# A decoder layer on one core: the embedding's projection moved from behind the output projection to the start and kept in DRAM, and the MLP's first two tiles cut by tokens around LN1's last transposes

## The chip, the cores and the metric

One core of a Trainium2 chip runs the kernel. The metric is the time of one execution on the device, in microseconds (us). TensorE (PE) multiplies, VectorE (DVE) and ScalarE (ACT) work element by element, GpSimd (POOL) does the small odd things and starts the accumulating transfers, and SyncE (SP) starts most other transfers between DRAM and the on-chip memory (SBUF). PE's results land in PSUM banks, from which DVE and ACT read them.

## The reference, cut to what matters

One layer on 512 tokens of width 1024, all in float32:

```python
h = layer_norm(x, ln_in_g, ln_in_b)
pool_in, qkv, z, beta, a, gate_a, gate_b = split(h @ w_in)
y_a = multiscale_pool(pool_in) ; y_b = gated_deltanet(qkv, z, beta, a)
mixed = sigmoid(gate_a) * y_a + sigmoid(gate_b) * y_b
h = layer_norm(alpha * h + mixed @ w_out, ln1_g, ln1_b)
r = alpha * h + square(relu(h @ w_up)) @ w_down
ple = sigmoid(r @ ple_gate_w) * (p @ ple_proj_w)
out = layer_norm(r + ple, ln2_g, ln2_b)
```

The change concerns `p @ ple_proj_w`: `p` is the token embedding (512 x 256), `ple_proj_w` is 256 x 1024. This product needs nothing but inputs and is first used in the last step but one.

## The kernel before

Float32 values are split into a high part that PE multiplies fast and a low part, and each product is three matmuls: high by high, high by low, low by high. A weight slab of 512 KB is loaded by SP into a `raw` buffer (three of them), ACT casts it to `hi`, DVE subtracts to get `lo` (`load`, lines 48 to 59; four buffers of each). `load` runs these two ahead of their turn, by `high_priority`. Activations live feature by feature in `act`, 8 blocks of 128 features by 512 tokens, high and low.

Until the MLP a scheduler orders each engine's instructions by the program's order and the priorities given; `issue_after` forces an order between two of them. From the MLP on, everything goes through the wrappers `oT`, `oV`, `oA`, `oS`, `oG`, which keep the order of the code on each engine.

**The start (lines 137 to 254).** PE runs 14 warm-up matmuls on the identity. SP loads `x` as eight halves of 256 KB (four tiles of 128 tokens), then the first weights. For each tile DVE takes the statistics (`stats`, lines 98 to 103), POOL works out the scale, and ACT normalises in place (line 213). PE transposes feature block by feature block (`ps_in`, line 228); behind two of these in block 3 stand four more warm-up matmuls. ACT applies gain and offset (`hf_in`, line 233), and ACT or DVE writes the high part, DVE the low part (lines 234, 235). PE then multiplies these features by the small beta/decay weights (`ps_ba`, lines 247 and 248) and the first k weights (`ps_k`, lines 66 to 68). `ps_bat` (line 254) follows the last of `ps_ba`.

**The middle.** Projections, DeltaNet by pairs of heads, pool mixer and gates follow. At lines 735 to 743 the token embedding is loaded (`ptok`), transposed by PE and split into `pT`. `tok_gemm` (from line 749) multiplies the mixed result by `w_out`; its callback `out_done` (from line 796) adds the residual, takes LN1's statistics, applies the norm into `res[t]`, and calls `to_features` (lines 109 to 119), which transposes `res[t]` into `act` through PSUM tiles `ps_l`. Behind `tok_gemm` stands the embedding's projection (lines 814 to 826): two weight halves, eight PSUM tiles `ps_pp`, 48 matmuls, and eight ACT copies into SBUF tiles `pproj`, where they stay until the end.

**The MLP (from line 831).** Eight chunks `c` of 512 hidden features. A chunk has four tiles of the up projection (`up_tile`), each 24 matmuls over all 512 tokens. Only the first two tiles of chunk 0 are cut into token halves, `HALVES`, 48 matmuls of 256 columns each. `even_block` and `odd_block` apply the squared ReLU on ACT and split it into `hid_a`, `hid_b` and `hid_s` on ACT and DVE. The down projection is a Strassen-like scheme with seven products of 2 x 2 blocks. Its right-hand sides are sums of quarters of `w_down`, built in place: `fetch` loads a quarter (`x`, `y`, `z`, `w`), and `onto` adds the next quarter onto it by an accumulating transfer that POOL issues, after ACT and DVE have split the former content (`split_dn`: `hi_dn` on ACT, `lo_dn` on DVE). In chunk 0 ACT also scales the four residual tiles (`alpha_h`). All lines that go through the wrappers carry the number 844 in the profile.

**The end.** After chunk 7 the last products are gathered into `res`, `features` transposes `res` into `act` (`ps_rt`), `gate_tile` multiplies by `ple_gate_w` (`ps_pg`), `embed` multiplies the sigmoid by `pproj`, and `finish` does LN2 and the output.

Of the kernel before, what the change touches and what calls it, by code (L numbers as in the profile page):

```python
# [33 lines left out]
def layer(tc, x, p, ln_in_g, ln_in_b, w_in, pool_w, pool_scale, conv_w, a_log, dt_bias, o_norm_w,  # L34
# [163 lines left out]


# [25 lines left out]
    for kb in range(KB):  # L225
        ps = pp1.tile([P, SEQ], F32, tag=("tp", "sc")[kb % 2], bufs=2, name=f"ps_in_{kb}")
        for t in range(NT):
            pe_last = T.transpose(ps[:, t * P:(t + 1) * P], xts[t][:, kb * P:(kb + 1) * P], ident)
# [505 lines left out]

    ptok = tp2.tile([P, NT, 256], F32, tag="ptok", bufs=1, name="ptok")
    dma(out=ptok, in_=p[0, 0].rearrange("(t p) c -> p t c", p=P))
    pT = tp2.tile([P, 2, 2, SEQ], F32R, tag="pT", bufs=1, name="pT")
    for kb in range(2):
        ps = pp2.tile([P, SEQ], F32, tag="tp", bufs=2, name=f"ps_pT{kb}")
        for t in range(NT):  # L740
            T.transpose(ps[:, t * P:(t + 1) * P], ptok[:, t, kb * P:(kb + 1) * P], ident)
        A.copy(pT[:, kb, 0, :], ps)
        V.tensor_tensor(out=pT[:, kb, 1, :], in0=ps, in1=pT[:, kb, 0, :].bitcast(F32), op=SUB)

# [68 lines left out]

    pproj = {}
    for half in range(2):
        hi, lo = load(ple_proj_w[0, :, 512 * half:512 * half + 512].rearrange("(a p) c -> p a c", p=P), 512,
                      f"pp{half}")
        for t in range(NT):
            ps = pp2.tile([P, 512], F32, tag="g", bufs=pp2g, name=f"ps_pp{half}{t}")
            for kb in range(2):  # L820
                ah, al = pT[:, kb, 0, t * P:(t + 1) * P], pT[:, kb, 1, t * P:(t + 1) * P]
                T.matmul(ps, ah, hi[:, kb, :], start=kb == 0, stop=False)
                T.matmul(ps, ah, lo[:, kb, :], start=False, stop=False)
                T.matmul(ps, al, hi[:, kb, :], start=False, stop=kb == 1)
            pproj[t, half] = ep.tile([P, 512], F32, tag="E", bufs=8, name=f"pproj{half}{t}")
            A.copy(pproj[t, half], ps)
# [345 lines left out]
```

## Time and profile before

| | us |
|---|---|
| runs | 852.21, 852.46, 853.06 |
| median | 852.46 |
| profiled execution | 852.83 |
| its span (granted TensorE clock 0.996) | 851.0 |
| PE busy | 833.2 (98%) |
| DVE busy | 605.9 (71%) |
| ACT busy | 404.0 (47%) |
| POOL busy | 90.0 (11%) |
| DRAM read, written | 95.56 MB, 2.10 MB |

The span goes from the first to the last instruction that the profiler recorded; the execution's own time is 1.83 us longer. A busy time counts instructions at work, not registers, branches or the issue of transfers. A row of a view gives an instruction's start and duration, its engine, its line in the kernel, the operation, and output and inputs by the program's names. What stands in brackets behind it is the engine's idle time just before it and what ended that. PE's matmuls overlap one another, so a row's duration is longer than the distance from one start to the next. The granted clock is the share of TensorE's full speed.

### The profile page before, as it was taken

How to read it: one execution, taken by the hardware profiler on the slowest of the kernel's cores; microseconds unless marked ns; L12 is line 12 of the kernel's file. 1: busy time of each engine (PE TensorE's matmuls, PEld its weight loads, DVE VectorE, ACT ScalarE, POOL GpSimd, SP SyncE). 2: the span in 40 equal slices, each digit the busy share in tenths (PEclk: the TensorE clock that was granted, in tenths of full speed). 3: DMA queues.
4: the chain of work that ended last, by engine and by line, in shares of the span. 5: the costliest groups of instructions: out<-in, count | busy, mean ns of one | idle time of the engine just before them, and what ended most of it. 6: DMA issues, size and time to landing. Idle time of an engine off the chain costs nothing.

```text
span 851.0 us, 12480 instructions
## 1 busy us (share of the span) xinstructions
PE 833.2 (98%) x4848; PEld 693.9 (82%) x4848; DVE 605.9 (71%) x1185; ACT 404.0 (47%) x628; POOL 90.0 (11%) x94
## 2 busy tenths in 40 slices
PE   7999999999999999999999999999999999999996
PEld 5787888888888888888888878888888888888785
DVE  8798968759866635569369394857576767667986
ACT  5566455465563634442207555353545453634510
POOL 4061000001000000110011111111111111010000
PEclk9999999999999999999999999999999999999999
DMA  6313222321321312265316647575757566654221
GB/s 204 99 53 96 83 69 54 97 75 50 84 73 33 109 47 75 81 211 159 125 50 217 155 128 174 140 172 139 179 138 190 133 166 163 156 127 123 75 75 49
DMA packets 73196, 98.45 MB, mean 116 GB/s; under 512 B 4537, under 2 KB 48946, under 8 KB 73138
## 3 DMA queue, kind: packets, MB, share of 16 engines
q1 hardware_dynamic: 64384, 80.87, 30.0%
q0 software_dynamic: 8704, 16.78, 11.9%
q8 instruction: 38, 0.62, 0.3%
q14 instruction: 20, 0.16, 0.1%
q10 hardware_dynamic: 50, 0.01, 0.0%
HBM read 95.56 MB, written 2.10 MB: 115 GB/s over the span
## 4 chain that ended last, share of the span: by engine, by line
PE 90%; DVE 5%; ACT 2%; DMA 1%; issue 1%; POOL 0%; SPq 0%; DVEq 0%; ACTq 0%; POOLq 0%
PE ps_up L844 19%; PE ps_dnx L844 5%; PE ps_pg L844 5%; PE ps_dn L844 5%; PE ps_dny L844 5%; PE ps_dnz L844 3%; PE ps_z L67 2%; PE ps_gb L66 2%; PE ps_z L66 2%; PE ps_ga L67 2%; PE ps_gb L68 2%; PE ps_gb L67 2%; PE ps_z L68 2%; PE ps_ga L66 2%; PE ps_ga L68 2%; PE ps_q L66 1%
## 5 line engine op out<-in xcount | busy, mean ns | idle before, releaser
L844 PE MATMUL ps_up<-act,hi_up 128*128 128x512 f32 x480 | 147.8, 389 | 0.0
L844 PEld LDWEIGHTS ps_up<-act,hi_up 128*128 128x128 f32 x480 | 90.0, 188 | 18.6
L844 PE MATMUL ps_up<-act,lo_up 128*128 128x512 f32 x240 | 93.4, 389 | 0.0
L844 ACT ACTIVATE r<-ps_up 128x512 f32<-128x512 f32 x32 | 19.0, 595 | 102.4 <-PE ps_up L844 99.5
L844 POOL DMA_DIRECT2D x<-in_w_down_dram x24 | 29.0, 1210 | 273.8 <-DVE lo_dn L844 273.8
L844 PEld LDWEIGHTS ps_up<-act,lo_up 128*128 128x128 f32 x240 | 45.0, 188 | 9.4
L844 DVE TENSOR_TENSOR lo_dn<-x,hi_dn 128x1024 fp32r<-128x1024 f32 x32 | 39.0, 1220 | 8.3 <-ACT hi_dn L844 8.3
L844 PE MATMUL ps_dnx<-hi_dn,hid_s 128*128 128x512 f32 x128 | 42.3, 391 | 0.0
L844 ACT CAST hi_dn<-x 128x1024 fp32r<-128x1024 f32 x32 | 33.5, 1048 | 12.2 <-PE ps_dn L844 9.0
L844 ACT CAST hid_s<-r 128x512 fp32r<-128x512 f32 x32 | 18.3, 618 | 41.5 <-DVE r L844 41.5
L844 DVE TENSOR_TENSOR hid_a<-r,hid_a 128x256 fp32r<-128x256 f32 x16 | 6.8, 426 | 41.4 <-ACT hid_a L844 41.4
L844 PE MATMUL ps_pg<-hi_pg,act 128*128 128x512 f32 (+1 forms) x128 | 35.9, 363 | 0.0
L844 DVE TENSOR_TENSOR hid_b<-r,hid_b 128x512 fp32r<-128x512 f32 x16 | 11.1, 692 | 34.0 <-ACT hid_b L844 34.0
L844 DVE TENSOR_TENSOR lo_up<-raw_up,hi_up 128x1024 fp32r<-128x1024 f32 x28 | 33.5, 1217 | 0.0
L844 DVE TENSOR_TENSOR r<-r 128x256 f32<-128x256 f32 x64 | 27.2, 425 | 2.2
L844 ACT CAST hi_up<-raw_up 128x1024 fp32r<-128x1024 f32 x28 | 28.6, 1046 | 0.0
L844 PEld LDWEIGHTS ps_dnx<-hi_dn,hid_s 128*128 128x128 f32 x128 | 23.9, 188 | 5.7 <-DVE hid_s L844 0.4
L844 DVE TENSOR_TENSOR hid_s<-r,hid_s 128x512 fp32r<-128x512 f32 x32 | 20.7, 689 | 11.0 <-ACT hid_s L844 11.0
L844 PEld LDWEIGHTS ps_pg<-hi_pg,act 128*128 128x128 f32 x128 | 23.1, 189 | 3.8
L844 PE MATMUL ps_dnx<-lo_dn,hid_s 128*128 128x512 f32 x64 | 24.9, 389 | 0.0
L577 POOL TENSOR_TENSOR rs<-rs,mhalf 128x4 f32<-128x4 f32 x8 | 9.0, 1131 | 150.0 <-DVE rs L576 150.0
L844 DVE TENSOR_TENSOR res<-ps_dnx,res 128x512 f32<-128x512 f32 x32 | 21.0, 685 | 4.7 <-PE ps_dnx L844 4.7
(734 smaller groups left out, 2397.2 us busy)
## 6 DMA issues: line engine op xcount, KB each, us to landing
raw_up<-in_w_up_dram SPq DMA_DIRECT2D x32, 512.0 KB, 7.9
x<-in_w_down_dram POOLq DMA_DIRECT2D x24, 512.0 KB, 6.1
raw_wo<-in_w_out_dram SPq DMA_DIRECT2D x8, 512.0 KB, 3.5
x<-in_w_down_dram SPq DMA_DIRECT2D x8, 512.0 KB, 9.3
z<-in_w_down_dram SPq DMA_DIRECT2D x8, 512.0 KB
y<-in_w_down_dram SPq DMA_DIRECT2D x8, 512.0 KB, 7.7
w<-in_w_down_dram SPq DMA_DIRECT2D x8, 512.0 KB, 3.5
y<-in_w_down_dram POOLq DMA_DIRECT2D x8, 512.0 KB, 8.8
```

The costliest lines, as they stand in the source:

```text
L66: T.matmul(ps, wh, ah, start=first, stop=False)
L67: T.matmul(ps, wh, al, start=False, stop=False)
L68: T.matmul(ps, wl, ah, start=False, stop=last)
L577: G.tensor_tensor(out=rs, in0=rs, in1=mhalf.to_broadcast([P, NT]), op=ALU.pow)
L844: return lambda *a, **k: tc.keep_in_program_order(op(*a, **k))
```

## The change

The load, transposition, split and projection of the embedding now stand at the start of the program, ahead of the loads of `x`. Each of the eight results is copied by ACT from PSUM into an SBUF tile of the pool `ep`, and SP writes it to a DRAM tile (`dp`, 256 KB each). In chunks 2 and 3 SP reads the eight tiles back into SBUF, where `embed` finds them. LN_in's statistics are put behind the last `lo_pp` on DVE by `issue_after`. The four warm-up matmuls in block 3 are gone.

At LN1, `out_done` transposes only the first two token tiles. The first two up tiles (`start`) run over the first 256 tokens; then the transposes of token tiles 2 and 3 follow through `features`, which keep the code's order; and the second halves of both up tiles come where the whole tiles stood. The first pair of up slabs is split without the head start of 300 in priority; the second pair is loaded raw and split after the first second half. The PSUM tiles `perm` are taken behind these transposes. At the end, the split of a gate slab (`gates`) and the gather of product 7 change places.

The diff, cut to its core:

```diff
     warm_up(ps_warm, 14)
+    dp = root.enter_context(tc.tile_pool(name="dp", bufs=8, space=bass.MemoryType.DRAM))
+    ptok = mxp.tile([P, NT, 256], F32, tag="big", name="ptok")
+    dma(out=ptok, in_=p[0, 0].rearrange("(t p) c -> p t c", p=P))
+    wraw = []
+    for half in range(2):
+        raw = wp.tile([P, 2, 512], F32, tag="raw", bufs=3, name=f"raw_pp{half}")
+        dma(out=raw, in_=ple_proj_w[0, :, 512 * half:512 * half + 512].rearrange("(a p) c -> p a c", p=P))
+        wraw.append(raw)
...
+    for kb in range(2):
+        ps = tps(f"ps_pT{kb}")
+        for t in range(NT):
+            T.transpose(ps[:, t, :], ptok[:, t, kb * P:(kb + 1) * P], ident)
+        ps = ps.rearrange("p t c -> p (t c)")
+        act_last = A.copy(pT[kb][0], ps)
+        vec_last = V.tensor_tensor(out=pT[kb][1], in0=ps, in1=pT[kb][0].bitcast(F32), op=SUB)
+    wpp = []
+    for half in range(2):
...
+        with tc.issue_after(act_last.ins), tc.issue_after(vec_last.ins):
+            act_last = A.copy(hi, wraw[half])
+            vec_last = V.tensor_tensor(out=lo, in0=wraw[half], in1=hi.bitcast(F32), op=SUB)
+        wpp.append((hi, lo))
+    st_last = vec_last
+    pproj = {}
+    def project(half):
+        hi, lo = wpp[half]
+        for t in range(NT):
+            ps = gps(f"ps_pp{half}{t}")
...
+            got = ep.tile([P, 512], F32, tag="E", bufs=8, name=f"ppc{half}{t}")
+            A.copy(got, ps)
+            pproj[t, half] = dp.tile([P, 512], F32, tag="pp", bufs=8, name=f"pproj{half}{t}")
+            dma(out=pproj[t, half], in_=got)
     xts = []
...
+    for half in range(2):
+        project(half)
...
-        with tc.issue_after(st_last.ins) if t else nullcontext():
+        with tc.issue_after(st_last.ins):
             st_last = stats(xts[t], f"in{t}", tp1, mv_in[:, t, :])
...
-            if kb == 3:
-                with tc.issue_after(pe_last.ins):
-                    warm_up(ps_warm, (2, 2, 0, 0)[t])
...
-            to_features(res[t], t, pp2, ("tp",), 2, "l1")
+            if t < 2:
+                to_features(res[t], t, pp2, ("tp",), 2, "l1")
...
-    ups = [slab(w_up[0], k0, c0, f"up0_{c0}{k0}") for c0 in (0, 256) for k0 in (0, 512)]
-    x, z, y, b22 = fetch(0, "x", 0, 0), fetch(0, "z", 1, 0), None, None
+    ups = [slab(w_up[0], k0, 0, f"up0_0{k0}", ahead=0) for k0 in (0, 512)]
+    raws = [raw_slab(w_up[0], 0, 256, 256, "up0_2560")]
+    x, z = fetch(0, "x", 0, 0), fetch(0, "z", 1, 0)
+    raws.append(raw_slab(w_up[0], 512, 256, 256, "up0_256512"))
     y, b22 = fetch(0, "y", 0, 1), fetch(0, "w", 1, 1)
+    start = [g3(f"ps_up00{i}") for i in range(2)]
+    for i in range(2):
+        up_tile(start[i], i, ups, HALVES[0])
+    for t in range(2, NT):
+        features(t, "l1")
+    perm = {i: [pp3.tile([P, SEQ], F32, tag="u", bufs=4, name=f"ps_dn{i}_{m}") for m in range(2)]
+            for i in (1, 6)}
...
-        ps = up_tile(c, 0, 0, ups[0:2])
         if fst:
+            ps = up_tile(start[0], 0, ups, HALVES[1])
+            ups += [split_up(raw, f"up0{n}") for n, raw in enumerate(raws)]
             w[1] = split_dn(x, f"{c}1")
             onto(x, c, 0, 1)
...
+        if c in (2, 3):
+            for t in range(NT):
+                got = ep.tile([P, 512], F32, tag="E", bufs=8, name=f"ppb{c - 2}{t}")
+                oS.dma_start(out=got, in_=pproj[t, c - 2])
+                pproj[t, c - 2] = got
...
-    gates = [[ups[0], split_up(raws[1], "pg01")], []]
     product(7, left, w[7], yb, True, True)
     gather(yb, 1, 1, SUB)
+    gates = [[ups[0], split_up(raws[1], "pg01")], []]
```

Three places show how it moves instructions. The first is PE at the end of the input transposes; `ps_in` is one feature block's transposes, `ps_pp` a tile of the projection, `ps_ba` and `ps_k` the first products on the features. Before, from the fifth block on:

```order
L228 MATMUL ps_in_242<-ident,x_106 128x128
L228 MATMUL ps_in_242<-ident,x_109 128x128
L228 MATMUL ps_in_242<-ident,x_112 128x128
L228 MATMUL ps_in_242<-ident,x_115 128x128
L247 MATMUL ps_ba<-act,hi_ba 32x512
L66 MATMUL ps_k_448<-act,hi_k_194 128x512
L248 MATMUL ps_ba<-act,hi_ba 32x512
L67 MATMUL ps_k_448<-act,hi_k_194 128x512
L68 MATMUL ps_k_448<-act,lo_k_195 128x512
L228 MATMUL ps_in_251<-ident,x_106 128x128
L228 MATMUL ps_in_251<-ident,x_109 128x128
L228 MATMUL ps_in_251<-ident,x_112 128x128
```

Now, from the projection's last matmuls on, which stand ahead of the eighth block:

```order
L174 MATMUL ps_pp_263<-hi_pp_136,pT_116 128x512
L175 MATMUL ps_pp_263<-lo_pp_137,pT_116 128x512
L176 MATMUL ps_pp_263<-hi_pp_136,pT_117 128x512
L274 MATMUL ps_in_387<-ident,x_140 128x128
L274 MATMUL ps_in_387<-ident,x_143 128x128
L274 MATMUL ps_in_387<-ident,x_146 128x128
L274 MATMUL ps_in_387<-ident,x_149 128x128
L284 MATMUL ps_crow<-ident,crow 128x96
L290 MATMUL ps_ba<-act,hi_ba 32x512
L291 MATMUL ps_ba<-act,hi_ba 32x512
L290 MATMUL ps_ba<-act,hi_ba 32x512
L291 MATMUL ps_ba<-act,hi_ba 32x512
```

Before, the products are mixed with the transposes of the later blocks; now all of them follow the last block, and the projection's matmuls stand between the transposes.

The second place is ACT from the last normalisation of `x` to the first `hf_in` tiles; `ppc` is the SBUF copy of a projection tile, `hi_k` a weight cast, `pcol` the columns of gains and offsets. Before:

```order
L213 ACTIVATE x_115<-x_115,nmr,rstd_in 128x512
L219 COPY pcol<-ps_prow 128x25
L233 ACTIVATE hf_in_203<-ps_in_198,pcol 128x512
L195 CAST hi_k_225<-raw_k_144 128x1024
L233 ACTIVATE hf_in_212<-ps_in_207,pcol 128x512
L233 ACTIVATE hf_in_221<-ps_in_216,pcol 128x512
L233 ACTIVATE hf_in_238<-ps_in_229,pcol 128x512
L234 CAST act<-hf_in_221 128x512
```

Now:

```order
L178 COPY ppc_215<-ps_pp_208 128x512
L259 ACTIVATE x_149<-x_149,nmr,rstd_in 128x512
L265 COPY pcol<-ps_prow 128x25
L178 COPY ppc_226<-ps_pp_219 128x512
L238 CAST hi_k_347<-raw_k_178 128x1024
L178 COPY ppc_237<-ps_pp_230 128x512
L276 ACTIVATE hf_in_325<-ps_in_320,pcol 128x512
L276 ACTIVATE hf_in_334<-ps_in_329,pcol 128x512
L276 ACTIVATE hf_in_343<-ps_in_338,pcol 128x512
L178 COPY ppc_248<-ps_pp_241 128x512
L276 ACTIVATE hf_in_356<-ps_in_351,pcol 128x512
L277 CAST act<-hf_in_343 128x512
```

Three copies of the projection and the cast `hi_k` have come in between the normalisations' end and the first `hf_in`, or just ahead of it, and another copy behind the third.

The third place is DVE at LN1's last token tile, from the aggregate to the first `lo_dn` of the MLP; `lo_up` and `lo_dn` are low parts of up and down weights, the rows into `act` the low parts of the transposed features. Before:

```order
L58 TENSOR_TENSOR lo_up_0512_4711<-raw_up_0512_4708,hi_up_0512_4710 128x1024
L789 BN_AGGR mv_l_4583<-st_l_4383 128x2
L58 TENSOR_TENSOR lo_up_2560_4717<-raw_up_2560_4714,hi_up_2560_4716 128x1024
L106 TENSOR_SCALAR rstd_l_4585<-mv_l_4583 128x1
L803 SCALAR_TENSOR_TENSOR y_4191<-y_4191,mv_l_4583,gb_l_4196 128x1024
L804 SCALAR_TENSOR_TENSOR res_4224<-y_4191,rstd_l_4585,gb_l_4196 128x1024
L119 TENSOR_TENSOR act<-ps_l_2_0_4515,act 128x4x128
L119 TENSOR_TENSOR act<-ps_l_2_1_4522,act 128x4x128
L58 TENSOR_TENSOR lo_up_256512_4723<-raw_up_256512_4720,hi_up_256512_4722 128x1024
L119 TENSOR_TENSOR act<-ps_l_3_0_4590,act 128x4x128
L119 TENSOR_TENSOR act<-ps_l_3_1_4597,act 128x4x128
L844 TENSOR_TENSOR lo_dn_4784<-x_4726,hi_dn_4783 128x1024
```

Now:

```order
L816 BN_STATS st_l_4484<-y_4309 128x6
L821 BN_AGGR mv_l_4670<-st_l_4484 128x2
L106 TENSOR_SCALAR rstd_l_4672<-mv_l_4670 128x1
L835 SCALAR_TENSOR_TENSOR y_4309<-y_4309,mv_l_4670,gb_l_4314 128x1024
L836 SCALAR_TENSOR_TENSOR res_4325<-y_4309,rstd_l_4672,gb_l_4314 128x1024
L863 TENSOR_TENSOR act<-ps_l_4761,act 128x4x128
L863 TENSOR_TENSOR act<-ps_l_4768,act 128x4x128
L863 TENSOR_TENSOR act<-ps_l_4775,act 128x4x128
L863 TENSOR_TENSOR act<-ps_l_4782,act 128x4x128
L863 TENSOR_TENSOR lo_up_4818<-raw_up_2560_4699,hi_up_4817 128x1024
L863 TENSOR_TENSOR lo_up_4822<-raw_up_256512_4705,hi_up_4821 128x1024
L863 TENSOR_TENSOR lo_dn_4826<-x_4701,hi_dn_4825 128x1024
```

The split of the second pair of up slabs, mixed with the norm and the transposed features before, now follows all of them, just ahead of the first `lo_dn`.

More of the change, by code (lines that the diff above doesn't have):

```diff
@@ L7 @@
-from contextlib import ExitStack, nullcontext
+from contextlib import ExitStack
 import concourse.bass as bass
@@ L732, in layer @@
     pp2.tile([P, SEQ], F32, tag="g", bufs=6, name="ps_g")
[L735 to L743, printed above, removed]
     def rslab(w, k0, c0, name, **kw):
@@ L811, in layer @@
     tok_gemm(w_out[0], lambda kb, i, t: mixed[kb][:, i, t * P:(t + 1) * P], _P2(), "g", "wo", out_done)
[L814 to L826, printed above, removed]
     ph2.close()
@@ L849, in g3 @@
         return pp3.tile([P, SEQ], F32, tag="g", bufs=4, name=name)
-    perm = {i: [pp3.tile([P, SEQ], F32, tag="u", bufs=4, name=f"ps_dn{i}_{m}") for m in range(2)]
-            for i in (1, 6)}
     def wide(name):
@@ L899, in split_up, with up_tile @@
         return split(raw, name, wp, ("whi", "wlo"))
-    def up_tile(c, j, i, gr):
-        ps = g3(f"ps_up{c}{j}{i}")
-        ms = slice(i * P, (i + 1) * P)
-        first = c == 0 and j == 0
-        for c0, c1 in (HALVES if first else ((0, SEQ),)):
-            for kb in range(KB):
-                hi, lo = gr[kb // 4]
-                for q, (w, h) in enumerate(((hi, 0), (hi, 1), (lo, 0))):
-                    (T if first else oT).matmul(ps[:, c0:c1], w[:, kb % 4, ms], act[:, kb, h, c0:c1],
-                                                start=kb == 0 and q == 0, stop=kb == KB - 1 and q == 2)
+    def up_tile(ps, i, gr, cut=(0, SEQ)):
+        ms, (c0, c1) = slice(i * P, (i + 1) * P), cut
+        for kb in range(KB):
+            hi, lo = gr[kb // 4]
+            for q, (w, h) in enumerate(((hi, 0), (hi, 1), (lo, 0))):
+                oT.matmul(ps[:, c0:c1], w[:, kb % 4, ms], act[:, kb, h, c0:c1],
+                          start=kb == 0 and q == 0, stop=kb == KB - 1 and q == 2)
         return ps
@@ L962, in gather, with features @@
                 oV.tensor_tensor(out=dst, in0=dst, in1=banks[m], op=SUB)
-    def features(t):
+    def features(t, name="rt"):
         for half in range(2):
-            ps = pp3.tile([P, 4, P], F32, tag="u", bufs=4, name=f"ps_rt{t}{half}")
+            ps = pp3.tile([P, 4, P], F32, tag="u", bufs=4, name=f"ps_{name}{t}{half}")
             for a in range(4):
@@ L994, in layer @@
         else:
+            ps = up_tile(g3(f"ps_up{c}00"), 0, ups[0:2])
             gather(yb, 1, 0)
@@ L1000, in layer @@
         r2, ha = even_block(c, 0, ps)
-        ps = up_tile(c, 0, 1, ups[0:2])
+        ps = up_tile(start[1], 1, ups[0:2], HALVES[1]) if fst else up_tile(g3(f"ps_up{c}01"), 1, ups[0:2])
         w[2] = split_dn(z, f"{c}2")
@@ L1014, in layer @@
         left[0] = odd_block(c, 0, ps, r2, ha)
-        ps = up_tile(c, 1, 0, ups[2:4])
+        ps = up_tile(g3(f"ps_up{c}10"), 0, ups[2:4])
         if fst:
@@ L1018, in layer @@
         r2, ha = even_block(c, 1, ps)
-        ps = up_tile(c, 1, 1, ups[2:4])
+        ps = up_tile(g3(f"ps_up{c}11"), 1, ups[2:4])
         if fst:
```

8 lines of the change are left out of this document (added).

## The prediction

> **What bounds the kernel now.** I began with the page's span and its busy line.
>
> ```profile
> span 851.0 us, 12480 instructions
> PE 833.2 (98%) x4848; PEld 693.9 (82%) x4848; DVE 605.9 (71%) x1185; ACT 404.0 (47%) x628; POOL 90.0 (11%) x94
> ```
>
> TensorE (PE) is busy nearly throughout, and the edit hardly changes its work, so the question is where it is *not* the limit. Next came the busy time by stretches; a row gives start:end, length, busy time of each engine, granted clock, DMA share, GB/s.
>
> ```profile
> 25.00:452.00 427.00, 424.95 (x2948) 354.86 (x2947) 307.38 (x754) 203.76 (x350) 36.87 (x31) 1.00 0.28 85
> 452.00:500.00 48.00, 47.67 (x260) 40.03 (x259) 31.34 (x44) 31.90 (x47) 6.49 (x5) 1.00 0.72 201
> 500.00:790.00 290.00, 290.00 (x1281) 240.14 (x1280) 196.33 (x269) 139.21 (x191) 33.91 (x28) 1.00 0.61 150
> ```
>
> ```profile
> 5.00:10.00 5.00, 2.65 (x22) 2.23 (x20) 4.55 (x11) 3.53 (x3) 2.92 (x8) 1.00 1.06 315
> 10.00:15.00 5.00, 2.97 (x21) 2.20 (x21) 3.83 (x8) 3.74 (x6) 2.42 (x5) 0.99 0.62 170
> 15.00:20.00 5.00, 5.00 (x22) 3.85 (x22) 4.28 (x7) 4.88 (x9) 0.00 (x0) 0.67 0.58 196
> ```
>
> PE alone sets the time from 25 to 452 and from 500 to 790: what delays it before 25 delays the end by as much. Before 15 PE idles about half the time. There x loads (DMA share 1.06), VectorE (DVE) takes the statistics, and ScalarE (ACT) normalises. So the front is a chain DMA, DVE, POOL, ACT, PE, and the moved projection uses the first four as well. At 452 to 500 PE is full, but its work there includes the projection, which leaves. Which other engine is nearly late there has to be read from the rows.
>
> **The front.** The chain of waits dates the input, and two groups the LN_in work (start, duration, engine, line; the bracket is the idle time before).
>
> ```profile
> 1.24 3.16 DMA x<-in_x_dram
> 4.78 4.95 DMA x<-in_x_dram
> ```
>
> ```profile
> 4.34 1.27 DVE L102 BATCH_NORM_STATS2 st_in<-x 128x6 f32<-128x512 f32 x2
> 10.48 0.21 DVE L103 BATCH_NORM_AGGREGATE mv_in<-st_in 128x2 f32<-128x12 f32 x1
> 12.32 0.82 ACT L213 ACTIVATE x<-x,nmr,rstd_in 128x512 f32<-128x512 f32 x1 [0.70 <-POOL nmr L210]
> 13.62 0.78 ACT L233 ACTIVATE hf_in<-ps_in,pcol 128x512 f32<-128x512 f32 x1 [0.41 <-PE ps_in L228]
> 21.64 0.78 ACT L233 ACTIVATE hf_in<-ps_in,pcol 128x512 f32<-128x512 f32 x1 [1.03 <-DVE act L235]
> ```
>
> ```profile
> 6.31 0.24 PE L218 MATMUL ps_prow<-ident,prow 25*128 25x25 f32 x1
> 25.09 0.39 PE L66 MATMUL ps_k<-act,hi_k 128*128 128x512 f32 x1
> 26.93 0.39 PE L68 MATMUL ps_k<-act,lo_k 128*128 128x512 f32 x1
> ```
>
> The projection's own operations have rows where they stand now.
>
> ```profile
> L57 ACT CAST hi_pp<-raw_pp x2: 1043/1046/1049, 449.3 to 450.2; 128x1024 fp32r<-128x1024 f32 x2
> L58 DVE TENSOR_TENSOR lo_pp<-raw_pp,hi_pp x2: 1206/1212/1217, 450.4 to 453.1; 128x1024 fp32r<-128x1024 f32 x2
> L826 ACT COPY pproj<-ps_pp x8: 574/588/603, 454.7 to 465.1; 128x512 f32<-128x512 f32 x8
> L742 ACT CAST pT<-ps_pT x2: 583/588/592, 409.0 to 409.5; 128x512 fp32r<-128x512 f32 x2
> L743 DVE TENSOR_TENSOR pT<-ps_pT,pT x2: 681/682/684, 409.7 to 410.3; 128x512 fp32r<-128x512 f32 x2
> ```
>
> *Bytes.* x's first tile lands at 4.40, its last half at 9.73: 6 halves in 5.33, 0.89 each. The token embedding and two weight halves (512 KB each, six halves in all) now go first on SP's queue, so x ends 5.3 later, at 15.0.
>
> *DVE.* The edit chains the statistics behind lo_pp. The warm-up matmuls run to about 6.3; the four-block transposes and two pT copies on ACT (0.59 each) reach 8.1, two hi_pp (1.05 each) 10.2, the second lo_pp (1.21) 11.4, some 0.1 of hand-over. Four tiles of statistics at 1.27 + 0.21 = 1.48 make 5.9: 17.4, against 10.69 before. That is 6.7 late, later than the bytes alone.
>
> *ACT.* Statistics to the last normalisation took 12.32 − 10.69 = 1.63, hence 19.0 and, with 0.82, 19.9. Before the first hf_in its list now holds two more projection copies (0.59 each) and a weight cast (1.05, formerly behind hf_in): with the small pcol copy, 22.3; hf_in ends about 23.1, where it ended at 14.40: 8.7 late. First to last hf_in took 8.02. Without the 1.03 wait and the cast, and with three copies inserted, it takes 8.02 − 1.03 − 1.05 + 1.77 = 7.7: the last ends at 30.8, 8.4 late.
>
> *PE.* All 40 matmuls of ba and the first k tile now stand behind the last transpose, where they were mixed with the transposes. The last transposes must wait for a PSUM slot that the fourth hf_in frees, and for the last projection tile: about 27.2. The two k rows are eight issues apart, 0.23 each, so 40 take 9.2: 36.4, against 27.3 before. **Term: +9.0**, bounds +8.4 (ACT's delay) and +9.5. Below these lies +5.3, if only bytes counted (a rival).
>
> What else is in the front costs nothing: the four removed warm-ups and PE's 48 projection matmuls (48 × 0.23 = 11.0) fall in PE's idle time; the eight DRAM writes (2 MB) fall at 12 to 32, beside 85 to 196 GB/s that nobody waits for later. The 2 MB read back falls in 500 to 790, DMA share 0.61, no PE wait; without that cover a 256 KB load is exposed by up to 3.2, as x's first.
>
> **Around LN1.** PE gives up 11.0 here, and only what DVE and ACT give up as well is a gain.
>
> ```profile
> 452.13 1.31 PE L822 MATMUL ps_pp<-hi_pp,pT 128*128 128x512 f32 x5
> 492.91 0.73 PE L844 MATMUL ps_dnz<-hi_dn,hid_b 128*128 128x512 f32 x2
> ```
>
> ```profile
> 453.08 1.21 DVE L58 TENSOR_TENSOR lo_pp<-raw_pp,hi_pp 128x1024 fp32r<-128x1024 f32 x1
> 467.63 1.23 DVE L844 TENSOR_TENSOR lo_dn<-x,hi_dn 128x1024 fp32r<-128x1024 f32 x1
> 469.49 1.40 POOL L844 DMA_DIRECT2D x<-in_w_down_dram  x1 [7.03 <-DVE lo_dn L844]
> 477.38 1.05 ACT L844 CAST hi_dn<-x 128x1024 fp32r<-128x1024 f32 x1 [3.26 <-DMA x<-in_w_down_dram]
> 492.17 0.69 DVE L844 TENSOR_TENSOR hid_b<-r,hid_b 128x512 fp32r<-128x512 f32 x1 [0.40 <-ACT hid_b L844]
> ```
>
> ```profile
> x<-in_w_down_dram POOLq DMA_DIRECT2D x24, 512.0 KB, 6.1
> ```
>
> Read the second fence as one path: lo_dn is done at 468.86; only then may the accumulating DMA write its buffer x; ACT waits 3.26 for that DMA until 477.38, and casts, residual scaling and activations follow in its fixed order; hid_b's low part is done at 492.86. PE's first matmuls on the late hid_b start at 492.91, five hundredths later. So PE and this path are tied at 492.9, and 11.0 less PE work buys only what the path gains.
>
> *The path.* From 453.08 to lo_dn's end DVE's list loses one operation, lo_pp (1.21); the two later up splits only change places with the transposed casts. The transposes and casts hang on PE and ACT hand-overs, of which I take 0.2 back: lo_dn ends 1.0 earlier. The DMA took 7.89 from issue to ACT's start; I keep that. From ACT's cast to hid_b is 15.5, unchanged, for the four residual scalings and all activations stay in it. **Term: −1.0.** Bounds: 0 if the transfer meets the raw slabs now loading without head start; −2.8 if it lands in the 6.1 that the 24 such transfers need in the middle (1.0 + 1.8).
>
> On 7.9 against 6.1 the Trainium skill bears ("DMA: Bandwidth & Descriptors", Issuing engines are not separate DMA queues): transfers started by different engines share the same 16 DMA engines and interleave. The trace agrees, with DMA share 0.72 and 201 GB/s at 452 to 500 beside 0.61 and 150 later; by it 7.9 stays, by the median the sum would be 1.8 lower.
>
> So PE's 11.0 turns into waits: after w_out it waits for t = 1's low part (453.08 + 1.21 + 0.68 = 455.0, from 452.13: 2.8), about 1 between LN1's last transposes and the second halves, and the rest, some 7, for hid_a and hid_b.
>
> **The tail.** The gate weights' split moves behind the last combination.
>
> ```profile
> 794.15 0.47 PE L844 MATMUL ps_dny<-hi_dn,hid_b 128*128 128x512 f32 x1 [1.30 <-DVE res L844]
> 801.60 1.28 DVE L844 TENSOR_TENSOR res<-ps_dny,res 128x512 f32<-128x512 f32 x2
> ```
>
> The 1.30 wait at 794.15 can go, but the features after it need the residuals that DVE finishes at 802.88, and the same DVE operations stand before them. Late next: those same residuals. **Term: 0**, bounds 0 and −1.2 (one split, as lo_pp's row).
>
> **Sum.** The profiled execution took 852.83 (span 851.0). 852.83 + 9.0 − 1.0 = 860.8. The median shown, 852.46, lies 0.37 below, so the forecast is 860.5. The terms' bounds give 852.46 + 8.4 − 2.8 = 858.1 to 852.46 + 9.5 = 862.0.
>
> **Rivals.** *B, the clock.*
>
> ```profile
> 15.83 0.63 PE L248 MATMUL ps_ba<-act,hi_ba 128*32 128x512 f32 x1
> 16.26 0.63 PE L67 MATMUL ps_k<-act,hi_k 128*128 128x512 f32 x1
> ```
>
> In 15 to 20 the granted clock was 0.67 and matmuls came 0.43 apart, after a stretch with PE busy 2.97 of 5. If PE's waits for hf_in do this again just ahead of the 40 matmuls, with the four warm-ups gone, one such stretch costs 5 × 0.33 = 1.6, two 3.3: 862.1 to 863.8. Against it: the projection's matmuls now fill those waits. It decides if PE idles as in 10 to 15. The Trainium skill ("TensorE: Matmul & The Clock Gate", Part 1: The HAM clock gate) says that the array falls to half clock after an idle window of some 3.4 us and returns after as much sustained work; by its rule half of 3.4, 1.7, is lost, 862.2. Chance 0.12.
>
> *C, the LN1 path lets go.* If the accumulating DMA is no longer waited for, or ACT gets its casts in earlier, PE keeps more of its 11.0; all of it less the 2.8 wait is 8.2. With the front at +9.0: 853.3 to 858.7, middle 856. Against it: ACT and PE are tied at 492.9, and no ACT work leaves the path. Chance 0.13.
>
> *D, faster.* The front costs only its bytes, 5.3, because DVE and ACT fit the pT and pp work in before x lands; and PE keeps 8.2 at LN1: 852.46 + 5.3 − 8.2 = 849.6. It decides when the front's delay is below what LN1 gives. Against it: DVE's statistics are chained, 5.9 from 11.4, and the same two engines carry both terms. Chance 0.09.
>
> *A, the forecast*, has 0.66. The range goes down into C's middle and up through B: 855 to 864. About 0.2% (1.7 us) is what a measurement of this kernel tells from no change. Faster by more is D and C's extreme, 0.10; within it the rest of C's low end, 0.04; slower 0.86.
>
> **What would show it.** Right: the last aggregate of LN_in near 17.6, first hf_in near 22.3, ps_bat near 36.5; PE idle some 10 within the first MLP block, with hid_a and hid_b as releasers; the first w_down accumulation near 468.5, relative to w_out's end. Wrong: aggregates ending by 16 or k matmuls ending by 33 (D's front); no PE waits for hid_b (C); matmuls 0.43 apart after 27 (B).

## The result, and the profile after

| | kernel before | changed kernel |
|---|---|---|
| median of the runs (us) | 852.76 | 863.27 |
| lowest and highest | 852.21, 854.18 | 862.41, 864.86 |
| profiled execution | 852.83 | 862.41 |
| its span | 851.0 | 860.4 |

The ratio of changed to before is 1.0123 with a 95% interval of 1.0103 to 1.0142: slower by 8.8 to 12.1, some 10.5. The forecast was 860.5 with a range of 855 to 864. In the two profiled executions the spans differ by 9.4; the medians differ by a good microsecond more, and the section on the hardware comes back to that. One execution of the experiments, of the LN1 part with the early accumulation, took 1043.29 at a mean granted clock of 0.752 and is left out of all medians, ranges and ratios.

The first lines of the changed kernel's profile:

```profile
span 860.4 us, 12497 instructions
PE 833.5 (97%) x4840; PEld 692.7 (81%) x4840; DVE 605.7 (70%) x1185; ACT 403.0 (47%) x628; POOL 90.0 (10%) x94
```

PE is busy for 0.3 longer (833.5 against 833.2), so all but 0.3 of the 9.4 is idle time of PE. The busy time by stretches shows where (start:end, length, busy time of each engine with the instruction count, granted clock, DMA share, GB/s):

```profile
15.00:20.00 5.00, 4.06 (x23) 3.25 (x24) 3.90 (x9) 5.00 (x8) 3.87 (x9) 1.00 0.62 220
20.00:25.00 5.00, 5.00 (x32) 4.30 (x31) 3.20 (x6) 5.00 (x9) 0.00 (x0) 1.00 0.87 263
...
40.00:461.00 421.00, 418.23 (x2915) 349.82 (x2913) 303.16 (x745) 199.79 (x344) 36.82 (x31) 1.00 0.28 84
461.00:510.00 49.00, 39.45 (x213) 32.18 (x213) 29.52 (x43) 26.07 (x37) 6.49 (x5) 0.97 0.65 171
510.00:800.00 290.00, 290.00 (x1281) 240.15 (x1280) 196.26 (x269) 138.69 (x191) 33.90 (x28) 1.00 0.62 157
```

Between 40 and 461 and between 510 and 800 PE sets the time as before. At 461 to 510 it now idles 9.5 of 49, where it idled 0.3 of 48. So the projection's 11.0 of PE went to the front, which is 9 longer, and most of the room that it left at LN1 stands empty.

**The front.** Rows of DVE, ACT and PE in the changed kernel; the last block has two rows of the kernel before:

```profile
17.02 0.21 DVE L103 BATCH_NORM_AGGREGATE mv_in<-st_in 128x2 f32<-128x12 f32 x1
...
21.54 2.14 ACT L276 ACTIVATE hf_in<-ps_in,pcol 128x512 f32<-128x512 f32 x3
28.91 0.78 ACT L276 ACTIVATE hf_in<-ps_in,pcol 128x512 f32<-128x512 f32 x1
```

```profile
15.73 0.66 PE L274 MATMUL ps_in<-ident,x 128*128 128x128 f32 x4 [1.28 <-ACT x L259]
...
26.36 0.60 PE L274 MATMUL ps_in<-ident,x 128*128 128x128 f32 x4
36.50 0.43 PE L297 MATMUL ps_bat<-ident,bat 32*128 32x32 f32 x4 [0.20 <-ACT bat L294]
```

```profile
8.53 0.66 PE L228 MATMUL ps_in<-ident,x 128*128 128x128 f32 x4 [1.99 <-ACT x L213]
27.52 0.43 PE L254 MATMUL ps_bat<-ident,bat 32*128 32x32 f32 x4 [0.20 <-ACT bat L251]
```

The last aggregate ends at 17.2 (forecast 17.4), the first hf_in begins at 21.5 (22.3) and the last ends at 29.7 (30.8), the last input transposes stand at 26.4 (27.2), and ps_bat at 36.50, where it stood at 27.52: 9.0 later, as forecast. Of these 9.0, PE's first transposes of x bring 7.2 (8.53 and 15.73); the stretch from there to ps_bat takes 20.8 instead of 19.0.

**Around LN1.** The path that the prediction followed, in the changed kernel:

```profile
475.43 1.22 DVE L863 TENSOR_TENSOR lo_dn<-x,hi_dn 128x1024 fp32r<-128x1024 f32 x1
477.28 1.40 POOL L863 DMA_DIRECT2D x<-in_w_down_dram  x1 [10.27 <-PE ps_up L863]
486.74 1.05 ACT L863 CAST hi_dn<-x 128x1024 fp32r<-128x1024 f32 x1 [8.23 <-DMA x<-in_w_down_dram]
501.55 0.69 DVE L863 TENSOR_TENSOR hid_b<-r,hid_b 128x512 fp32r<-128x512 f32 x1 [0.39 <-ACT hid_b L863]
```

And PE's waits there, from the list of waits (engine, line, tile and what it waited for: total, times, longest):

```profile
PE ps_dn L863 <- ACT hid_a L863: 4.4, 1, 4.4
PE ps_up L863 <- DVE act L119: 2.5, 1, 2.5
PE ps_dnz L863 <- ACT hid_b L863: 1.7, 1, 1.7
```

The shift from the front is still there when DVE writes the first low part of token tile 0, before and now:

```profile
447.55 0.69 DVE L119 TENSOR_TENSOR act<-ps_l,act 128x512 fp32r<-128x512 f32 x1
456.36 0.69 DVE L119 TENSOR_TENSOR act<-ps_l,act 128x512 fp32r<-128x512 f32 x1
```

That is 8.81 later; lo_dn is 7.80 later (467.63 and 475.43): 1.0 won, as forecast. But the accumulating transfer, 9.46 from issue to ACT's start against 7.89, takes 1.6 back, and hid_b's low part is 9.38 later (492.17 and 501.55). ACT waits 8.2 for that one transfer, PE 4.4 and 1.7 for what ACT does behind it.

**The tail.** PE's 1.30 wait at 794.15 has become 0.17, and a wait of 0.87 for the residuals has come right behind it:

```profile
802.41 0.47 PE L863 MATMUL ps_dny<-hi_dn,hid_b 128*128 128x512 f32 x1 [0.17 <-DVE res L863]
811.73 1.97 PE L863 MATMUL ps_rt<-ident,res 128*128 128x128 f32 x16 [0.87 <-DVE res L863]
```

### The profile page after: what moved, and what is told of

Same layout as the page of the kernel before. It is cut to its first block, busy times and chain, and to the rows that moved or that the text cites. A ratio compares the mean times of both kernels' runs of the same rounds, so it can differ in the third digit from the quotient of the medians.

```text
span 860.4 us, 12497 instructions
## 1 busy us (share of the span) xinstructions
PE 833.5 (97%) x4840; PEld 692.7 (81%) x4840; DVE 605.7 (70%) x1185; ACT 403.0 (47%) x628; POOL 90.0 (10%) x94
## 4 chain that ended last, share of the span: by engine, by line
PE 86%; DVE 6%; ACT 4%; issue 3%; DMA 1%; POOL 0%; DVEq 0%; ACTq 0%; POOLq 0%
PE ps_up L863 18%; PE ps_dnx L863 5%; PE ps_dn L863 5%; PE ps_dny L863 5%; PE ps_pg L863 4%; PE ps_dnz L863 2%; PE ps_z L67 2%; PE ps_gb L66 2%; PE ps_z L66 2%; PE ps_ga L67 2%; PE ps_gb L68 2%; PE ps_gb L67 2%; PE ps_ga L66 2%; PE ps_z L68 2%; PE ps_ga L68 2%
## 5 line engine op out<-in xcount | busy, mean ns | idle before, releaser
L863 PE MATMUL ps_up<-act,hi_up 128*128 128x512 f32 (+1 forms) x544 | 159.9, 377 | 3.4 <-DVE act L119 2.5
L863 PEld LDWEIGHTS ps_up<-act,hi_up 128*128 128x128 f32 x544 | 100.1, 188 | 22.7 <-DVE act L119 2.7
L863 PE MATMUL ps_up<-act,lo_up 128*128 128x512 f32 (+1 forms) x272 | 102.4, 377 | 0.0
L863 PEld LDWEIGHTS ps_up<-act,lo_up 128*128 128x128 f32 x272 | 51.2, 188 | 9.4
L863 ACT CAST hi_dn<-x 128x1024 fp32r<-128x1024 f32 x32 | 33.6, 1051 | 17.2 <-PE ps_dn L863 9.0
L863 DVE TENSOR_TENSOR lo_up<-raw_up,hi_up 128x1024 fp32r<-128x1024 f32 x30 | 35.8, 1216 | 0.0
L863 ACT CAST hi_up<-raw_up 128x1024 fp32r<-128x1024 f32 x30 | 30.7, 1050 | 0.0
L863 DVE TENSOR_TENSOR r<-r 128x256 f32<-128x256 f32 x64 | 27.2, 425 | 2.2
L863 PE MATMUL ps_dn<-hi_dn,hid_a 128*128 128x512 f32 x64 | 23.4, 407 | 4.4 <-ACT hid_a L863 4.4
```

The lines of the kernel that those rows point to most:

```text
L863: return lambda *a, **k: tc.keep_in_program_order(op(*a, **k))
```

## The experiments

The theory: the front is late by what now comes ahead of x, and at LN1 the path DVE, accumulating transfer, ACT sets the time, so that PE's freed 11.0 buy nothing. The rivals: PE's sum decides throughout; the token halves hide or cost something by themselves; the bytes alone are the front. Every ratio below is to the kernel before, run beside the experiment; the number in brackets behind a median is the range, behind a ratio its 95% interval.

### One move against the path: the accumulation early

```diff
+    w = {1: split_dn(x, "01")}
+    onto(x, 0, 0, 1)
     for t in range(2, NT):
         features(t, "l1")
...
             ups += [split_up(raw, f"up0{n}") for n, raw in enumerate(raws)]
-            w[1] = split_dn(x, f"{c}1")
-            onto(x, c, 0, 1)
```

> The changed kernel with one move: chunk 0's first split of x and the accumulating transfer onto it stand ahead of the transposes of token tiles 2 and 3. In the changed kernel's trace ACT is idle from 461.4 to 470.1 and DVE from 468.3 to 470.8, and x was loaded from 458.5 on, so the split fits there and the transfer is issued near 470.1 instead of 477.3. Theory (the path over the accumulating transfer ate PE's time at LN1): ACT's second split of x starts near 479 to 480 instead of 486.7, PE's waits for hid_a (4.4) and hid_b (1.7) go, 5 to 6 faster than the changed kernel: 857 to 858. Rival 1 (ACT's and DVE's own queues set the pace there, the transfer only fills their idle time): within 1 of the changed kernel, 862 to 864.

Measured: 856.1 (853.6 to 857.7), ratio 1.0034 (1.0022 to 1.0046): 7.2 below the changed kernel's 863.27, or 7.6 by the two ratios, since the two kernels did not run beside each other. POOL issued the transfer at 470.43, and ACT's second split of x no longer waits for it:

```profile
477.66 1.04 ACT L863 CAST hi_dn<-z 128x1024 fp32r<-128x1024 f32 x1
478.61 1.05 ACT L863 CAST hi_dn<-x 128x1024 fp32r<-128x1024 f32 x1
```

No bracket stands behind either row: ACT runs on without a wait, 8.1 earlier than in the changed kernel. PE's waits for hid_a and hid_b are gone, and PE is busy 45.55 of 49 at 461 to 510. So the transfer was what kept PE waiting. The gain is even larger than the two waits together (6.1); the section on the hardware shows where most of the rest is.

### The LN1 part alone, with the accumulation late and early

The second of these two kernels has the same edit as above, on top of the first.

> The LN1 part of the change (and the move at the end) alone: the projection is computed in the middle as before, with its 11.0 of PE, and no front. Theory (path over the accumulating transfer): the projection's matmuls and the first token halves now stand ahead of the transposes of tiles 2 and 3 on PE, so these come some 8 later than in the changed kernel, and the path with them; PE has no other work to put there: +6 to +9 on the kernel before, 859 to 862. Rival (PE bound: the sum of PE's work is that of before, so nothing changes): within 1.5 of before, 851.5 to 854.

Measured: 861.9 (861.1 to 862.2), ratio 1.0102 (1.0087 to 1.0117), +8.9.

> The LN1 part alone (861.9, projection in the middle) with the early accumulation. Theory (the path over the accumulating transfer made the +8.9 of that kernel): the transfer is issued about 7 earlier, PE's waits for hid_a (4.3) and hid_b (1.7) go, 854 to 856, within 0.3% of the kernel before; PE is then the bound again. Rival (the order of the token halves itself costs): 859 or above.

Measured: 852.69 (851.9 to 853.6), ratio 1.0001 (0.9991 to 1.0011): the kernel before again, and 1.3 to 3.3 better than expected. In the first of the two the wait list and ACT show the same stop as the changed kernel's, though its front is the old one and PE has 11.0 more work ahead of it:

```profile
PE ps_dn L845 <- ACT hid_a L845: 4.3, 1, 4.3
PE ps_dnz L845 <- ACT hid_b L845: 1.7, 1, 1.7
```

```profile
485.61 1.05 ACT L845 CAST hi_dn<-x 128x1024 fp32r<-128x1024 f32 x1 [8.16 <-DMA x<-in_w_down_dram]
```

This rules out that PE's sum decides by itself: with unchanged work on PE, an order that delays the first accumulation cost 8.9, and one that issues it earlier gave all of that back. Not all of the 8.9 is waiting: PE's four waits there sum to 6.9, and in the three stretches 496 to 498, 502 to 504 and 504 to 506 PE is busy throughout at a granted clock of 0.50, 0.51 and 0.64, which takes another 2.7 (its span is 9.3 longer than that of the kernel before). In this kernel, with the transfer early, the token halves cost nothing.

### The front alone

> The front of the change alone: embedding projected at the start and kept in DRAM, but at LN1 and at the end the order of the kernel before (token halves behind all transposes, second pair of up slabs split early). Theory (the path over DVE's list and the accumulating transfer decides, PE's token halves fill time that is not on it): the front's +9.0 stays, DVE's list at LN1 is shorter by the two lo_pp (2.4), so as fast as the changed kernel or up to 2.5 faster: 860.5 to 863.5. Rival (the halves hide LN1's waits from PE): without them PE waits 5 or more longer, 868 or above.

Measured: 861.21 (860.5 to 862.4), ratio 1.0096 (1.0079 to 1.0113), 2.1 below the changed kernel. Without the halves PE waits at LN1's transposes themselves:

```profile
466.47 1.94 PE L116 MATMUL ps_l<-ident,res 128*128 128x128 f32 x8 [4.22 <-DVE act L119]
472.26 1.94 PE L116 MATMUL ps_l<-ident,res 128*128 128x128 f32 x8 [3.85 <-DVE res L836]
```

8.1 in these two, where the changed kernel has 9.5 in five. Behind the first of them the granted clock is 0.50 up to 476, over 5.7 of PE's busy time, which costs 2.8 more: together PE loses nearly all of the 11.0 that it was freed of. The halves move most of PE's wait from LN1 to behind the transfer; they remove none of it. The front costs 8.2 alone and the LN1 part 8.9, but together they cost 10.5 and not 17.1: PE waits in the same stretch in all three kernels, for 8.1, 6.9 and 9.5.

### The bytes ahead of x

```diff
+    more = [mxp.tile([P, DM], F32, tag="big", name=f"more{i}") for i in range(3)]
+    dma(out=more[0].rearrange("p (t c) -> p t c", c=256), in_=p[0, 0].rearrange("(t p) c -> p t c", p=P))
+    for half in range(2):
+        dma(out=more[1 + half].rearrange("p (a c) -> p a c", c=512),
+            in_=ple_proj_w[0, :, 512 * half:512 * half + 512].rearrange("(a p) c -> p a c", p=P))
     xts = []
```

> The kernel before, with the 1.5 MB of token embedding and projection weights loaded ahead of x into tiles that nobody reads; the rest is as before, so the projection is still computed in the middle. It prices the bytes alone. Theory (six halves at 0.89 each, DVE and ACT otherwise free): +5.3, about 858; the first hf_in starts near 18.9 instead of 13.6. Of the front's +9.0 then 3.7 are left for the engines' work. Rival (the bytes are all of it): +9, about 862. Rival (the loads overlap well enough): under +3.

Measured: 858.25 (856.4 to 859.5), ratio 1.0059 (1.0041 to 1.0077), +5.2 by the medians. The profiled execution was the fastest of its four, and in it less was late:

```profile
14.58 0.21 DVE L103 BATCH_NORM_AGGREGATE mv_in<-st_in 128x2 f32<-128x12 f32 x1
```

```profile
30.98 0.43 PE L259 MATMUL ps_bat<-ident,bat 32*128 32x32 f32 x4 [0.20 <-ACT bat L256]
```

The last aggregate is 4.1 later than before, ps_bat 3.5. So by this kernel 3.5 to 5.2 of the front's 9.0 are the bytes, and 4 to 5.5 the projection's work. The price holds a little of the clock: PE's granted clock is 0.64 at 10 to 15, with PE busy for 2.52, and 0.68 at 15 to 20, where the kernel before has 0.99 and 0.67 and the changed kernel 1.00.

### What of that work: ACT's copies, or PE

Two kernels, each run once, so that their times have no interval; ps_bat is the answer. First the copies, in nearly the same order of the engines (one of ACT's casts moves up by two places). The output of this kernel leaves the projection out:

```diff
-            A.copy(got, ps)
+            A.copy(got[:, 0:32], ps[:, 0:32])
...
-            dma(out=pproj[t, half], in_=got)
+            dma(out=pproj[t, half][:, 0:32], in_=got[:, 0:32])
...
-                oS.dma_start(out=got, in_=pproj[t, c - 2])
+                oS.dma_start(out=got, in_=xin[:, t, 0:512])
```

> The changed kernel with ACT's eight copies of projection tiles cut from 512 to 32 columns (and the DRAM writes with them; the tiles read back in chunks 2 and 3 come from x instead, so the output leaves the projection out). Every engine's order at the front is that of the changed kernel. It asks what makes the front's +9.0 late once x is there. Rival theory, the prediction's own step (ACT's list from the normalisations to the last hf_in is the chain): eight copies shorter by about 0.45 take 3 to 4 out of it, ps_bat comes at 33 to 34 instead of 36.5, the time falls by 3. Theory from the changed kernel's trace (PE works without a gap from 15.7 on, so PE's own sum is the end of the front): at most the 1.3 wait for x at 15.7 goes, ps_bat at 35.2 to 36.7.

```profile
36.34 0.43 PE L297 MATMUL ps_bat<-ident,bat 32*128 32x32 f32 x4
```

36.34 against 36.50: the gain of 3 to 4 that the prediction's chain by ACT's list would give did not come. The test is weaker than planned, for ACT waits for x between the copies: its last hf_in starts only 1.06 earlier (27.85 instead of 28.91), and five other profiles with the changed kernel's front have ps_bat at 36.13 to 37.29, so a gain below 1 could not be seen. What speaks more strongly against ACT's list is PE in the changed kernel: from 15.7 to 36.0 it is busy for 20.06 of 20.30, and its list of waits has no wait for hf_in. (The span of this one execution, 862.9, is 2.5 above the changed kernel's by what happens at LN1, as the section on the hardware shows.)

Then PE:

```diff
-                T.matmul(ps, ah, hi[:, kb, :], start=kb == 0, stop=False)
-                T.matmul(ps, ah, lo[:, kb, :], start=False, stop=False)
-                T.matmul(ps, al, hi[:, kb, :], start=False, stop=kb == 1)
+                T.matmul(ps, ah, hi[:, kb, :], start=kb == 0, stop=kb == 1)
```

> The changed kernel with one matmul in three of the projection (high by high only; the output's projection is less exact): 16 matmuls instead of 48 at the front, 7.3 less PE work, ACT's and DVE's work the same. The scheduler then mixes ps_ba and ps_k with the input transposes again, as in the kernel before, and puts the copies earlier. Theory (PE's own sum ends the front): what PE saves counts until DVE's statistics and ACT's chain are next: ps_bat at 32.5 to 34 instead of 36.5, 2.5 to 4 faster than the changed kernel, 859 to 861. Rival (ACT's chain, or the bytes, end the front): ps_bat 36 or later, no gain.

The expectation missed: ps_bat at 36.58, 865.5 in its one execution (in which the clock fell at LN1 too). PE did have 7.3 less to do, but it waited for x (2.9 in all) and for pcol (1.2), and then worked slowly:

```profile
15.00:20.00 5.00, 2.10 (x13) 1.20 (x13) 3.94 (x10) 4.72 (x6) 3.83 (x11) 1.00 1.03 369
20.00:25.00 5.00, 3.48 (x15) 2.52 (x14) 3.57 (x6) 4.44 (x8) 0.54 (x1) 0.55 0.98 334
25.00:30.00 5.00, 5.00 (x25) 3.95 (x24) 4.97 (x10) 4.36 (x7) 0.00 (x0) 0.76 0.35 101
```

The granted clock was 0.55 and 0.76 where it is 1.00 in the changed kernel. At 3.48 and 5.00 busy that is 0.45 × 3.48 + 0.24 × 5.00 = 2.8 lost, about what was to be gained. This is rival B's price, 1.6 to 3.3, found where PE idles, not where the projection keeps it busy. Whether PE's sum alone ends the changed kernel's front is therefore not settled by this kernel; the next one fits it.

### A better front

> The kernel with the early accumulation (856.1), and another order at the front: ACT and DVE split the first weight half ahead of the token embedding's copies, and ACT normalises x only behind the second projection copy, the later tiles behind the third and fourth. In the changed kernel PE waits there 1.5 for hi_pp and 0.5 for lo_pp and 1.3 for x at 15.7, and from then on it is busy without a gap worth naming. Theory (once the bytes are there, PE's own sum sets the front): only the waits ahead of 15.7 can be won; about 1 of the 2.0 and 1 of the 1.3: ps_bat near 34.7 instead of 36.6, 1.5 to 2 faster, 854 to 855. Rival (ACT's queue from the statistics to the last hf_in sets the front, as the prediction had it): the copies now stand ahead of the normalisations, so ps_bat comes no earlier or later, 856 to 858.

> The kernel with the early accumulation and the new front order, and two more moves: the second weight half's low part is made by POOL (idle there) instead of DVE, and at LN1 the second up slab's low part stands behind the transposed low parts of token tile 1, for which PE waits 2.5. Theory (what PE still waits for at the front and at LN1 is time on the end's path): ps_bat near 34, the wait at LN1 1.2 shorter, 852.5 to 854, the same as the kernel before within the measurement. Rival 1 (POOL's subtraction slows DVE's statistics, with which it shares time): no better than the new front order alone, 854 to 856. Rival 2 (PE finds the low part of the second slab late): the 2.5 wait comes back inside the first up tile.

The first of them, on the early accumulation, changes only the order:

```diff
+    act_last, vec_last = split_pp(0)
     for kb in range(2):
         ps = tps(f"ps_pT{kb}")
...
-        act_last = A.activation(a, a, AF.Identity, bias=nm, scale=rstd)
+        with tc.issue_after(copies[(1, 2, 2, 3)[t]].ins):
+            act_last = A.activation(a, a, AF.Identity, bias=nm, scale=rstd)
```

The second adds POOL for one subtraction, and `issue_after(lows[-1].ins)` around the second up slab's low part (`lows` holds the low parts of token tiles 0 and 1):

```diff
-                V.tensor_tensor(out=lo, in0=wraw[half], in1=hi.bitcast(F32), op=SUB))
+                (G if half else V).tensor_tensor(out=lo, in0=wraw[half], in1=hi.bitcast(F32), op=SUB))
```

Measured: 855.67 (853.5 to 856.3), ratio 1.0029 (1.0015 to 1.0042), and 852.83 (851.5 to 854.0), ratio 0.9998 (0.9989 to 1.0007). ps_bat, in the first and in the second:

```profile
35.30 0.43 PE L304 MATMUL ps_bat<-ident,bat 32*128 32x32 f32 x4 [0.20 <-ACT bat L301]
```

```profile
34.56 0.43 PE L306 MATMUL ps_bat<-ident,bat 32*128 32x32 f32 x4 [0.20 <-ACT bat L303]
```

Against the early accumulation (ps_bat at 36.68) the new order won 1.4 at ps_bat (1.9 expected) and 0.4 in the median (1.5 to 2 expected, so a miss, and within the intervals of the two ratios no gain at all); its profile has the slow clock behind the wait of 2.5 at LN1, as the kernel of the next section does. The other two moves won 2.8 more: 0.7 at ps_bat, 1.1 of that wait (1.4 is left), and the slow clock behind it, which is not in this profile. POOL's subtraction took 2.40 where DVE needs 1.21, and DVE's statistics were not longer for it (1.23 to 1.28 beside it). At 461 to 510 PE is busy 47.84 of 49. So the moved projection can be made to cost nothing, but no version here beats the kernel before: what the middle gives, the front takes.

### The neighbours of the transfer

```diff
     y, b22 = fetch(0, "y", 0, 1), fetch(0, "w", 1, 1)
+    nxt0 = [fetch(1, "x", 0, 0), fetch(1, "z", 1, 0)]
...
-            nxt = [fetch(c + 1, "x", 0, 0), fetch(c + 1, "z", 1, 0)]
+            nxt = nxt0 if fst else [fetch(c + 1, "x", 0, 0), fetch(c + 1, "z", 1, 0)]
```

> The changed kernel, with chunk 1's first two w_down quarters (x and z, 512 KB each) loaded in chunk 0 right behind chunk 0's own four, about 14 ahead of the first accumulating transfer, where the changed kernel issues them 0.8 to 1.3 ahead of it. It prices the contention that the prediction put at nothing: the transfer took 9.46 from issue to ACT's start, against 7.89 in the kernel before, where those two loads were issued 2.0 to 2.6 ahead. Theory (the 1 MB shares the 16 DMA engines with the transfer): ACT's second split of x starts 7.5 to 8 behind the issue, 1.5 to 2 faster than the changed kernel, 861 to 862. Rival (the transfer is slow for a reason of its own, reading and writing its target, or because of the up slabs that remain): 9.4 again, 863.

```profile
479.49 1.40 POOL L863 DMA_DIRECT2D x<-in_w_down_dram  x1 [11.71 <-PE ps_up L863]
```

```profile
486.62 1.05 ACT L863 CAST hi_dn<-x 128x1024 fp32r<-128x1024 f32 x1 [5.89 <-DMA x<-in_w_down_dram]
```

The transfer took 7.13, against 9.46 in the changed kernel and 9.21 to 9.81 in the five other profiles that issue these two loads 0.8 to 1.3 ahead of it: the two loads had cost it some 2.3. The front alone issues them 8 to 9 ahead, and there ACT found the transfer done 5.99 behind its issue. But the time did not fall: 863.4 (861.8 to 863.4), ratio 1.0119 (1.0104 to 1.0133). POOL issued 2.2 later. 0.8 of that is a later front in this execution (ps_bat 37.3). The other 1.4 PE lost in the first token halves, behind its wait of 2.5, where the granted clock was

```profile
464.00:466.00 2.00, 1.48 (x7) 1.48 (x8) 1.97 (x5) 0.00 (x0) 0.00 (x0) 0.60 1.02 325
466.00:468.00 2.00, 2.00 (x12) 2.00 (x12) 1.53 (x4) 0.00 (x0) 1.45 (x1) 0.55 1.04 388
```

and not 1.00 as in the changed kernel. Later PE waits 3.0 for hid_b instead of 1.7, and at 502 to 504 the clock is 0.50. So the mechanism is right for the transfer; the expected gain is a miss, for which the profiled execution shows these reasons, and the other three, which were not profiled, are left open.

### A filled wait, and the changed kernel again

```diff
+            if fst and j:
+                for _ in range(24):
+                    oT.matmul(xb[0][:, 0:P], ident, ident, start=True, stop=True)
             product(1, left, w[1], perm[1], fst, lst, (j,))
```

> The changed kernel with 24 matmuls of the identity by itself (128 columns, some 0.15 each, 3.6 in all; their result is overwritten) in the 4.4 that PE waits for the second hid_a. In the changed kernel's trace and in others with that wait the granted clock falls to 0.50 right behind it, for 2.5 to 10, in part over matmuls that nothing hides. Theory (the wait costs twice, by itself and by the clock behind it, for a length that differs from run to run): with PE at work in the wait the clock stays at 1.00 through 497 to 508 and the median is 1 to 2.5 below that of the changed kernel in the same call. Rival (the slow matmuls are hidden by the wait for hid_b that follows): within 0.5 of the changed kernel.

> The changed kernel again, unchanged, for the comparison beside it: 862.4 to 864.9 as before; the granted clock between 497 and 508 is 0.50 for some length that need not be that of the first profile.

Measured: 866.49 (865.1 to 868.0), ratio 1.0158 (1.0143 to 1.0173), and for the changed kernel beside it 864.79 (863.1 to 866.9), ratio 1.0145 (1.0122 to 1.0169). The filler did not fill the wait:

```profile
498.00 7.25 PE L863 MATMUL ps_dnx<-ident 128*128 128x128 f32 x48 [3.29 <-ACT r L863]
```

It waited 3.29 for ACT to be done with the former content of the PSUM tile that it writes, and then took 7.25, twice the estimate: the profile has 48 rows for the 24 matmuls, and the granted clock was 0.61 and 0.71 up to 503. Its front is later too in this execution (ps_bat at 37.29). So this kernel does not tell what a PE without the wait would gain, and the expected 1 to 2.5 stay open; a filler that PE could start at once was not tried.

## Why the prediction was right, point by point

**The front, +9.0: right in size, half right in cause.** ps_bat moved by 9.0, and the stations on the way (aggregate, first and last hf_in, last transposes) were met within 1.1. The first part of the chain holds: DVE's statistics end 6.5 later (forecast 6.7), and PE's transposes of x begin 7.2 later. Behind that, ACT's list was not what bound: PE waits for no hf_in from 15.7 on, and with shorter copies ps_bat stayed (36.34). The failing sentence is that PE's 48 projection matmuls "fall in PE's idle time". 30 of them stand behind 15.7, where the transposes of x begin: 30 × 0.23 = 6.9 of PE time. The stretch to ps_bat is nevertheless only 1.8 longer, because PE's waits of the kernel before (2.4 in the transposes), its warm-up matmuls there and its slow clock at 15 to 20 (1.6) are gone. That the size came out is in part luck: the forecast by ACT's list, 36.4, and the end of PE's own work, 36.5, happen to lie together.

**The bytes, +5.3 as a lower bound:** 3.5 in one execution, 5.2 in the medians. The rate of 0.89 per half of x was taken from a stretch that moves less: 315 GB/s at 5 to 10 in the kernel before, 391 in the changed kernel.

**LN1, −1.0: the mechanism right, the size and sign wrong.** The path was named and lo_dn came 1.0 earlier; PE's 11.0 turned into waits (9.5), with hid_a and hid_b as releasers. Wrong was to keep 7.89 for the transfer ("I keep that"). It took 9.46, which carries the term beyond its bound of 0. The next chunk's loads, issued 2.0 to 2.6 ahead of it before, now came 0.8 to 1.3 ahead; the prediction's own condition for 0, the raw slabs, was not the one. With these loads moved away it took 7.13. The measured term is 9.38 − 8.81 = +0.6. The upper end of the sum should have had room for that.

**The tail, 0: right.** The wait all but went, and 0.87 came back 9 later in the program, in the residuals named.

**The sum.** Forecast span 851.0 + 8.0 = 859.0, measured 860.4; the transfer's 1.6 covers the difference of 1.4. The median lies about 1 higher still.

**The rivals.** D (faster) asked that DVE and ACT fit the projection's splits in before x lands, and that LN1 give PE its time; neither held in the changed kernel, but the early accumulation shows that the second could for the most part (PE idles for 3.45 of 49 there). C's condition, the transfer no longer waited for, was met by that experiment, and its time, 856.1, is the value given for C. B was placed at the wrong hole: the front stayed at clock 1.00, and the clock fell at LN1.

## What to carry to other kernels

Moving PE work into an idle stretch can move the idle stretch: ask what bound the place it leaves. If a DMA and two other engines were just in time there, as here, PE's freed time comes back as a wait, and the first thing to move is the transfer's issue, not more PE work. Work put "into the wait for the input" cost two things here: the bytes that it brings, which go ahead of the input, and what was not done of it when the input arrived.
